# Attention scores of a hybrid decoder's mixer issued in pairs of heads on the two halves of TensorE's rows, with the mixer's order written by hand

## The chip, the core and the metric

The kernel runs on one core of a Trainium2 chip. The metric is the time of one execution on the device in microseconds, lower is better. The core has TensorE (PE) for matmuls, which reads SBUF and writes PSUM, VectorE (DVE), ScalarE (ACT), GpSimd (POOL), and SyncE (SP), which here issues the loads of the weights. Each engine takes its instructions in the order in which the program lists them; between engines, semaphores hold an instruction back until its inputs are there.

## The reference

Two layers, 256 tokens, width 1024, float32. Each layer is a half-step SwiGLU block, a mixer, and a second half-step SwiGLU block; a final RMS norm follows. The change is in the mixer alone:

```python
h = rms_norm(x, norm_mix[l])
qa, ka, va, qb, kb, vb, xc, gc = _split_cols(h @ w_in[l])
# A: 4 query heads, 2 key/value heads of 64, causal window 128, one sink logit per head
out_a = swa_sink_mixer(rope(qa), rope(ka), va, attn_sinks[l])
# B: 6 heads of 64, three dilated windows joined by their softmax denominators
out_b = dilated_mixer(rope(qb), rope(kb), vb)
# C: 384 channels, causal convolution over 4 tokens, gated linear recurrence, times gelu(gc)
out_c = rglru_mixer(xc, gc, conv_w[l], ...)
x = x + concat(out_a, out_b, out_c) @ w_out[l]
```

## The kernel before

Activations stand as columns of tokens in blocks of 128 channels (`xT`), split into a rounded part and a remainder (`hi`, `lo`); a weight piece of up to 128x1024 is loaded by SP into `raw` (`piece`, L123), rounded to `hi` on ScalarE (L130) and its remainder `lo` taken on VectorE (L132). A projection or a feed-forward product is three matmuls for each block of 128 input channels: hi times hi, hi times lo, lo times hi. Five `raw` tiles and fourteen `hi`/`lo` tiles let the weights run ahead of TensorE.

The mixer (L645) is a list of steps, `PLAN` (L20). `xc` and `gc` project C's two branches into channel rows (three PSUM banks each); `qb`, `kb`, `vb` project B's queries, keys and values and `pa` all of A's, with tokens in rows (one bank for each half of the tokens); `cg` and `cs` are C's gates and its recurrence, `co` its last product. `B1s0` is a score step of B for the second half of the tokens (h = 1), `B1p0` the transposes of one tile of probabilities, its copy to SBUF and its products with the values, `B1f` the division by the denominators and the transpose into `PT`; A's steps are named in the same way. `woB` and `woCA` multiply `PT` by `w_out` and add to `xT`. C's `gelu` stands at the end of the step `gc` (L776).

A head has 64 channels, so its scores, `q` times `k`, use 64 of TensorE's 128 rows: even heads of B and A's first key head the lower half, the others the upper half (`g`, L833 to L835). They are plain float32 products and each is recorded as two matmuls (20 head products in a layer, 40 records). A score step takes one PSUM bank (tag `at`) and heads of one half alone; A has two steps for each h, B two for h = 0 and four for h = 1. Then VectorE adds the mask and takes the row maxima (L838), ScalarE takes the exponentials (L847).

The steps are written in the order of `PLAN`, but a scheduler places each engine's instructions: the written order is their priority, and an instruction whose inputs it expects to be late lets later ones pass. `behind(ins)` (L120) pins instructions to come after `ins` on the same engine. PSUM has eight banks: four `mm`, two `at`, two `tp` (transposes). `LO` = 3: the last three input blocks of an output product are taken column block by column block (L941, L942).

Of the kernel before, what the change touches and what calls it, by code (L numbers as in the profile page):

```python
# [11 lines left out]
F32 = mybir.dt.float32  # L12
# [26 lines left out]
def hybrid_trunk(ctx: ExitStack, tc: tile.TileContext, a: dict, out: bass.AP):  # L39
# [397 lines left out]
    def gT(h, g, n, hi, lo):  # L437

        ps = bank("tp", "gT")
        for j in range(n // P):  # L440
            nc.tensor.transpose(ps[:, j * P:(j + 1) * P], g[:, j * P:(j + 1) * P], ident)
        split(hi, lo, ps[:, :n].rearrange("p (k t) -> p k t", t=P))

# [201 lines left out]
    def mixer(l, norm, nxt):  # L645
# [46 lines left out]

        def project(o, n, name):
            bs = None
            for k, w in w_in_pieces(o, n):
                if bs is None:
                    bs = [bank("mm", name)[:, :n] for _ in range(NH)]
                with behind_stats(k):
                    mac([(k, [(norm.parts(h, k), [(bs[h], w)]) for h in range(NH)])], KD)
            return bs  # L700

        def project_T(o, n, name, tags):

            bs = None
            for k, (wh, wl) in w_in_pieces(o, n):
                if bs is None:
                    bs = [bank(t, name)[:, :S] for t in tags]
                xh, xl = (norm.both(k)[:, o:o + S] for o in (0, S))
                with behind_stats(k):
                    for i, b in enumerate(bs):  # L710
                        wi, wj = (p[:, i * P:(i + 1) * P] for p in (wh, wl))
                        nc.tensor.matmul(b, wi, xh, start=(k == 0), stop=False)
                        nc.tensor.matmul(b, wi, xl, start=False, stop=False)
                        nc.tensor.matmul(b, wj, xh, start=False, stop=(k == KD - 1))
# [13 lines left out]
        def c_conv():  # L728
            xc = project_T(oC, CW, "xc", TAG_XC)
# [41 lines left out]
        def c_gelu():  # L771
            gc = project_T(oC + CW, CW, "gc", TAG_GC)
# [3 lines left out]
            A.activation(ge, ge, AF.Gelu_apprx_tanh)  # L776
# [31 lines left out]
        def q_k(ps, h, nh, dst, groups=None):  # L808
            r = rope(ps, h, nh, groups)
            n = nh * HD // P  # L810
            tp = bank("tp", "qkT")
            for c in range(n):
                nc.tensor.transpose(tp[:, c * P:(c + 1) * P], r[:, c * P:(c + 1) * P], ident)
            copy("qk", dst[:, :, h * P:(h + 1) * P], tp[:, :n * P].rearrange("p (c t) -> p c t", c=n))

        class Attend:


            def __init__(self, h, heads, vs, mask, sinks):
                self.h, self.heads, self.vs, self.mask, self.sinks = h, heads, vs, mask, sinks  # L820
                self.nk = (h + 1) * P
                self.nh = sum(len(b) for b in heads)
                st = act.tile([P, 4, 8], F32, tag="st", bufs=4, name="st")
                self.mx, self.nm, self.ls, self.ri = (st[:, i] for i in range(4))
                self.slot = [sum(len(b) for b in heads[:i]) for i in range(len(heads))]
                self.sm = [None] * len(heads)
                self.ob = None

            def scores(self, gi):
                group, j, nk, mx, nm = self.heads[gi], self.slot[gi], self.nk, self.mx, self.nm  # L830
                h, n = self.h, len(group)
# [4 lines left out]
                sm = act.tile([P, 512], F32, tag="sm", bufs=NSM, name="sm")  # L836
                for s in range(n):
                    V.tensor_tensor_reduce(out=sm[:, s * nk:(s + 1) * nk], in0=sb[:, s * nk:(s + 1) * nk],  # L838
                                           in1=self.mask, scale=1.0, scalar=NEG, op0=ALU.add, op1=ALU.max,
                                           accum_out=mx[:, j + s:j + s + 1])  # L840
                if self.sinks is None:
                    V.tensor_scalar(nm[:, j:j + n], mx[:, j:j + n], -SC, None, op0=ALU.mult)
                else:
                    V.scalar_tensor_tensor(nm[:, j:j + n], mx[:, j:j + n], -SC, self.sinks[1][:, j:j + n],
                                           op0=ALU.mult, op1=ALU.min)
                for s in range(n):
                    A.activation(sm[:, s * nk:(s + 1) * nk], sm[:, s * nk:(s + 1) * nk], AF.Exp, scale=SC,  # L847
                                 bias=nm[:, j + s:j + s + 1], accum_out=self.ls[:, j + s:j + s + 1])
                self.sm[gi] = sm

            def pv(self, gi):
                h, sm = self.h, self.sm[gi]
                if self.ob is None:
                    self.ob = bank(TAG_O, "o")
                tp = bank("tp", "pT")
                n = len(self.heads[gi]) * self.nk
                for b in range(n // P):
                    nc.tensor.transpose(tp[:, b * P:(b + 1) * P], sm[:, b * P:(b + 1) * P], ident)
                pT = act.tile([P, 512], F32, tag="pT", bufs=2, name="pT")
                copy("pT", pT[:, :n], tp[:, :n])  # L860
                for s, (i, g, q, k) in enumerate(self.heads[gi]):
                    for kb in range(h + 1):
                        b = s * (h + 1) + kb
                        nc.tensor.matmul(self.ob[:, i * HD:(i + 1) * HD], pT[:, b * P:(b + 1) * P], self.vs[kb][i],
                                         start=(kb == 0), stop=(kb == h))

            def finish(self):
                nh, ls, ri, ob, mx = self.nh, self.ls, self.ri, self.ob, self.mx
                if self.sinks is not None:
                    V.tensor_tensor(mx[:, :nh], self.sinks[0], self.nm[:, :nh], op=ALU.add)  # L870
                    A.activation(mx[:, :nh], mx[:, :nh], AF.Exp)
# [3 lines left out]
                order = [i for group in self.heads for i, *_ in group]  # L875
                if order == list(range(nh)):
                    V.tensor_tensor(o.rearrange("p (n d) -> p n d", d=HD),
                                    ob[:, :nh * HD].rearrange("p (n d) -> p n d", d=HD),
                                    ri[:, :nh, None].to_broadcast([P, nh, HD]), op=ALU.mult)
                else:  # L880

                    v = lambda z: z[:, :nh * HD].rearrange("p (n g d) -> p g n d", g=2, d=HD)
                    V.tensor_tensor(v(o), v(ob), ri[:, :nh].rearrange("p (g n) -> p g n", g=2)[:, :, :, None]
                                    .to_broadcast([P, 2, nh // 2, HD]), op=ALU.mult)
# [8 lines left out]
        def a_in():  # L893
            dst = qkA()
            pa = project(oA, (AQ + 2 * AKV) * HD, "pa")
            for h in range(NH):
# [3 lines left out]
                q_k(pa[h][:, :nq * HD], h, nq, dst, (AKV, AG))  # L900
            C["qkA"] = dst

        def a_attend(h):
# [3 lines left out]
            return Attend(h, heads, va, K["mA"][h], (K["sink"][:, sl], K["nsink"][:, sl]))  # L907

        def b_in(j):
            dst = QB[j][:, :NP * S].rearrange("p (c t) -> p c t", c=NP)  # L910
            pb = project(oB + j * NB, NB, "pb")
# [4 lines left out]
        def b_v():  # L916
            pb = project(oB + 2 * NB, NB, "vb")
# [5 lines left out]
        def b_attend(h, q, k):  # L923
            hd = lambda i: (i, i % 2, q[:, i // 2], k[:, i // 2])
            per = 512 // ((h + 1) * P)
            heads = []
            for g in range(2):
                for i0 in range(0, NP, per):
                    heads.append([hd(2 * i + g) for i in range(i0, min(i0 + per, NP))])
# [101 lines left out]
```

## Time and profile before

| | |
|---|---|
| three runs | 944.31 us median, 944.14 to 946.62 |
| profiled execution | 943.66 us, of which the span of its instructions is 941.9 us |
| PE busy | 933.2 us, 99% of the span, 7572 matmuls |
| DVE busy | 661.7 us, 70% |
| ACT busy | 501.9 us, 53% |
| SP's weight queue (q1) | 168.32 MB, 58.0% of the DMA engines' span |
| PE's granted clock | 0.998 of 2.4 GHz |
| first layer's mixer, first `xc` to last `wout` matmul | 190.15 to 291.08 us |
| second layer's mixer | 651.74 to 752.67 us |

Matmuls are pipelined: the duration of one reaches into the next, so the time that one costs is read from the distance between starts, not from its own duration. In a timeline, a line stands for a run of like instructions (xcount).

### The profile page before, as it was taken

Reading aid. Unit: us, or ns where it says so; the run is one execution under the profiler, and the core shown is the slowest. Engines: PE = TensorE matmul, PEld = TensorE weight load, DVE = VectorE, ACT = ScalarE, POOL = GpSimd, SP = SyncE. Lnnn points to the kernel's source line nnn. Section 1 sums busy time; section 2 is a strip of 40 time slices with the busy share of each in tenths; the row PEclk is TensorE's granted clock in tenths of the full one; section 3 lists DMA queues with packets and bytes.
Section 4 is the critical chain, followed back from the end, with each engine's and each line's share of the span. In section 5 each row is a group of like instructions: output and inputs, shape, how many; then the busy total and the mean of one; then the engine's idle time right before and its main releaser. Section 6 shows DMA issues by size and latency. Waiting matters only on the chain.

```text
span 941.9 us, 18771 instructions
## 1 busy us (share of the span) xinstructions
PE 933.2 (99%) x7572; PEld 908.8 (96%) x7572; DVE 661.7 (70%) x1155; ACT 501.9 (53%) x769; POOL 60.2 (6%) x107
## 2 busy tenths in 40 slices
PE   9999999999999999999999999999999999999997
PEld 8999999999899999999999999999988999999886
DVE  6787766999678767766477767565995975656544
ACT  7545554555577545554455545444475675555530
POOL 4000001011102000001000000011100100000000
PEclk9999999999999999999999999999999999999999
DMA  8886674665246665565756666654741755665631
GB/s 287 235 250 193 180 220 148 187 188 154 79 146 202 196 205 183 180 222 167 215 159 202 201 206 195 203 178 121 224 137 46 234 180 180 197 207 201 202 112 45
DMA packets 134406, 171.13 MB, mean 182 GB/s; under 512 B 5820, under 2 KB 106256, under 8 KB 134320
## 3 DMA queue, kind: packets, MB, share of 16 engines
q1 hardware_dynamic: 133184, 168.32, 58.0%
q0 software_dynamic: 528, 0.57, 0.5%
q8 instruction: 59, 0.97, 0.4%
q10 hardware_dynamic: 608, 1.06, 0.3%
q14 instruction: 27, 0.22, 0.1%
HBM read 168.88 MB, written 1.05 MB: 180 GB/s over the span
## 4 chain that ended last, share of the span: by engine, by line
PE 98%; issue 1%; DMA 1%; SPq 0%; DVE 0%; POOLq 0%; POOL 0%
PE gate L467 9%; PE gate L468 8%; PE gate L469 8%; PE up L467 8%; PE up L469 8%; PE up L468 8%; PE down L468 6%; PE down L467 6%; PE down L469 6%; PE down L616 2%; PE down L615 2%; PE down L617 2%; PE scores L834 2%; PE wout L946 2%; PE wout L947 2%; PE wout L948 2%
## 5 line engine op out<-in xcount | busy, mean ns | idle before, releaser
L132 DVE TENSOR_TENSOR lo<-raw,hi 128x1024 fp32r<-128x1024 f32 (+2 forms) x334 | 388.6, 1173 | 113.5 <-ACT hi L130 113.2
L130 ACT ACTIVATE hi<-raw 128x1024 fp32r<-128x1024 f32 (+2 forms) x334 | 335.6, 1018 | 167.0 <-PE down L468 60.9
L467 PE MATMUL gate<-x,hi 128*128 128x256 f32 x704 | 194.7, 277 | 0.1
L468 PE MATMUL gate<-x,hi 128*128 128x256 f32 x704 | 193.9, 276 | 0.0
L467 PE MATMUL up<-x,hi 128*128 128x256 f32 x704 | 193.6, 275 | 0.0
L468 PE MATMUL up<-x,hi 128*128 128x256 f32 x704 | 193.5, 275 | 0.0
L469 PE MATMUL gate<-x,lo 128*128 128x256 f32 x704 | 193.3, 275 | 0.0
L469 PE MATMUL up<-x,lo 128*128 128x256 f32 x704 | 193.3, 275 | 0.0
L467 PE MATMUL down<-g,hi 128*128 128x256 f32 x528 | 145.3, 275 | 0.0
L468 PE MATMUL down<-g,hi 128*128 128x256 f32 x528 | 145.2, 275 | 0.0
L469 PE MATMUL down<-g,lo 128*128 128x256 f32 x528 | 145.1, 275 | 0.0
L467 PEld LDWEIGHTS gate<-x,hi 128*128 128x128 f32 x704 | 132.3, 188 | 0.4 <-ACT x L376 0.4
L468 PEld LDWEIGHTS gate<-x,hi 128*128 128x128 f32 x704 | 132.2, 188 | 0.0
L468 PEld LDWEIGHTS up<-x,hi 128*128 128x128 f32 x704 | 132.1, 188 | 0.0
L469 PEld LDWEIGHTS up<-x,lo 128*128 128x128 f32 x704 | 132.1, 188 | 0.0
L467 PEld LDWEIGHTS up<-x,hi 128*128 128x128 f32 x704 | 132.0, 188 | 0.0
L469 PEld LDWEIGHTS gate<-x,lo 128*128 128x128 f32 x704 | 131.9, 188 | 0.0
L136 ACT ACTIVATE g<-gu 128x256 fp32r<-128x256 f32 x88 | 36.6, 418 | 148.3 <-DVE gu L481 124.5
L467 PEld LDWEIGHTS down<-g,hi 128*128 128x128 f32 x528 | 99.1, 188 | 0.1
L468 PEld LDWEIGHTS down<-g,hi 128*128 128x128 f32 x528 | 99.1, 188 | 0.0
L469 PEld LDWEIGHTS down<-g,lo 128*128 128x128 f32 x528 | 99.0, 188 | 0.0
L480 DVE TENSOR_TENSOR gu<-up,half 128x256 f32<-128x256 f32 x66 | 27.7, 420 | 46.1 <-PE up L469 46.0
(228 smaller groups left out, 1323.8 us busy)
## 6 DMA issues: line engine op xcount, KB each, us to landing
raw<-ffn_down SPq DMA_DIRECT2D x88, 512.0 KB, 4.6
raw<-ffn_gate SPq DMA_DIRECT2D x87, 512.0 KB, 4.8
raw<-ffn_up SPq DMA_DIRECT2D x87, 512.0 KB, 5.0
raw<-w_in SPq DMA_DIRECT2D x40, 384.0 KB, 3.8
raw<-w_out SPq DMA_DIRECT2D x12, 512.0 KB, 3.7
raw<-w_in SPq DMA_DIRECT2D x8, 512.0 KB, 4.8
raw<-w_out SPq DMA_DIRECT2D x8, 256.0 KB, 2.8
xr<-x SPq DMA_DIRECT2D x4, 256.0 KB, 4.2
```

Of the source, the lines that this page charges most:

```text
L130: nc.scalar.activation(hi[:, :m], raw[:, :m], AF.Copy)
L132: nc.vector.tensor_tensor(lo[:, :m], raw[:, :m], hi[:, :m].bitcast(F32), op=ALU.subtract)
L136: nc.scalar.activation(hi, v, AF.Copy)
L467: nc.tensor.matmul(b, wh, both[:, :S], start=first, stop=False)
L468: nc.tensor.matmul(b, wh, both[:, S:], start=False, stop=False)
L469: return nc.tensor.matmul(b, wl, both[:, :S], start=False, stop=last)
L480: V.tensor_tensor(u, bs[1], half, op=ALU.mult)
L615: nc.tensor.matmul(b, gh, wh, start=first, stop=False)
L616: nc.tensor.matmul(b, gh, wl, start=False, stop=False)
L617: return nc.tensor.matmul(b, gl, wh, start=False, stop=last)
L834: nc.tensor.matmul(sb[:, s * nk:(s + 1) * nk], q[g * HD:(g + 1) * HD, h * P:(h + 1) * P], k[g * HD:(g + 1) * HD, :nk], start=True, stop=True)
L946: nc.tensor.matmul(bs[j], wi, PT[:, k, 0], start=(i == 0), stop=False)
```

## The change

Scores: a step takes two `at` banks, one for each half of the rows, and goes through its heads by turns, lower half, upper half (`banks`, a list of two lists of heads). A has one such step for each h, B one for h = 0 (three pairs) and two for h = 1 (two pairs, then one): five steps in a layer instead of ten. The tiles of probabilities are filled by head number, so B has two and three of them, A one and two. The sink's exponential is taken at the end of A's score step instead of in `finish`.

Order: the step `p` is taken apart into `p` (transposes and copy) and `o` (products with the values). Projections, and `out_stage`, are generators that stop after two input blocks, or between their parts; each naming in `PLAN` runs one part. `C["pe"]` holds the last matmul so far of the projections and output products (or of a `gT`), and scores, transposes and value products are pinned behind it. A's query and key transposes (`aT0`, `aT1`) leave `a_in`, which now comes ahead of `vb`. The gelu is a step of its own (`gl`), pinned on ScalarE behind the last exponential of A. `o` tiles move from `at` to `mm`; an output product has two banks of each.

The core of the diff (left out: `whole`, which runs a generator to its end; `to_channels`, split from `q_k`; the same `yield` and `C["pe"]` in `project_T`; the regrouping of heads in `a_attend` and `b_attend`; `go_on`, which runs a step's next part):

```diff
-PLAN = ("xc qb kb cg B1s0 vb B0s0 B0s1 B0p0 B0p1 pa B1s2 B1s1 cs A0s0 B1s3 B1p0 B0f A0s1 B1p2 B1p1 A1s0 B1p3 "
-        "A1s1 A0p1 A0p0 gc A1p0 B1f woB A1p1 A0f A1f co woCA").split()
-TAG_GATE, TAG_SCORES, TAG_O, TAG_WO = 'at', 'at', 'at', 'mm'
-TAG_XC, TAG_GC = ('mm', 'at', 'mm'), ('at', 'mm', 'mm')
+PLAN = ("xc qb kb cg pa pa pa B0s0 pa B1s0 vb B0p0 B0p1 B1s1 cs vb aT0 vb aT1 A0s0 vb gc B0o0 B0o1 B1p0 B1p1 "
+        "gc B1o0 B1o1 B1p2 B0f gc B1o2 A0p0 gc B1f A0o0 A1s0 gl woB A1p0 A1p1 A0f woB A1o0 A1o1 co "
+        "woCA A1f woCA woCA woCA").split()
+TAG_GATE, TAG_SCORES, TAG_O, TAG_WO = 'at', 'at', 'mm', ('mm', 'mm', 'at', 'at')
+TAG_XC, TAG_GC = ('mm', 'at', 'mm'), ('mm', 'mm', 'mm')
...
         def project(o, n, name):
...
             for k, w in w_in_pieces(o, n):
+                if k and k % 2 == 0:
+                    yield
...
-                    mac([(k, [(norm.parts(h, k), [(bs[h], w)]) for h in range(NH)])], KD)
+                    C["pe"] = mac([(k, [(norm.parts(h, k), [(bs[h], w)]) for h in range(NH)])], KD)
...
         def c_gelu():
-            gc = project_T(oC + CW, CW, "gc", TAG_GC)
+            gc = yield from project_T(oC + CW, CW, "gc", TAG_GC)
...
-            A.activation(ge, ge, AF.Gelu_apprx_tanh)
...
             def scores(self, gi):
-                sb = bank(TAG_SCORES, "scores")
-                for s, (i, g, q, k) in enumerate(group):
-                    nc.tensor.matmul(sb[:, s * nk:(s + 1) * nk], q[g * HD:(g + 1) * HD, h * P:(h + 1) * P],
-                                     k[g * HD:(g + 1) * HD, :nk], start=True, stop=True)
+                sb = [bank(TAG_SCORES, "scores") for _ in banks]
+                for s in range(max(len(b) for b in banks)):
+                    for t, group in zip(sb, banks):
+                        if s < len(group):
+                            i, g, q, k = group[s]
+                            at[i] = t[:, s * nk:(s + 1) * nk]
+                            with behind(C["pe"]):
+                                nc.tensor.matmul(at[i], q[g * HD:(g + 1) * HD, h * P:(h + 1) * P],
+                                                 k[g * HD:(g + 1) * HD, :nk], start=True, stop=True)
...
+                if self.sinks is not None:
+                    V.tensor_tensor(mx[:, sl], self.sinks[0][:, sl], nm[:, sl], op=ALU.add)
+                    C["exp"] = A.activation(mx[:, sl], mx[:, sl], AF.Exp)
+
+            def pT(self, gi):
+                sm, heads = self.sm[gi]
+                tp = bank("tp", "pT")
+                n = len(heads) * self.nk
+                for b in range(n // P):
+                    with behind(C["pe"]):
+                        nc.tensor.transpose(tp[:, b * P:(b + 1) * P], sm[:, b * P:(b + 1) * P], ident)
...
         def out_stage(ks, last):
             for c in range(HC):
+                if c:
+                    yield
...
-                for i, j in order:
+                for ij, (i, j) in enumerate(order):
+                    if ij and ij == (n - LO) * KC:
+                        yield
...
+            elif nm == "gl":
+                with behind(C["exp"]):
+                    A.activation(C["ge"], C["ge"], AF.Gelu_apprx_tanh)
+            elif nm == "aT":
+                h = int(arg)
+                to_channels(C["rA"][h], h, nq, C["qkA"], C["pe"])
```

## Rows read from the trace of the kernel before

**Rows 1.** Waits of PE over the whole span: total us, times, longest.

```profile
PE warm L115 <- POOL ident masks.py:199: 1.4, 1, 1.4
PE xT L371 <- DMA xr<-x: 0.6, 1, 0.6
```

**Rows 2.** The page's part 4, the chain that ended last, by engine.

```profile
PE 98%; issue 1%; DMA 1%; SPq 0%; DVE 0%; POOLq 0%; POOL 0%
```

**Rows 3.** Groups by form, the score matmuls: xcount | busy us, mean ns.

```profile
L834 PE MATMUL scores<-mixed 64*128 64x256 f32 x40 | 11.8, 407 | 0.0
...
L834 PE MATMUL scores<-mixed 64*128 64x128 f32 x40 | 6.4, 287 | 0.0
```

**Rows 4.** PE's timeline at B0s1: start us, us, instruction.

```profile
238.51 0.40 PE L431 MATMUL pa<-hi,x 128*128 128x512 f32 x1
238.84 0.93 PE L834 MATMUL scores<-mixed 64*128 64x128 f32 x6
239.70 0.50 PE L432 MATMUL pa<-lo,x 128*128 128x512 f32 x1
240.04 0.40 PE L434 MATMUL pa<-hi,x 128*128 128x512 f32 x1
240.27 0.39 PE L431 MATMUL pa<-hi,x 128*128 128x512 f32 x1
```

**Rows 5.** PE's timeline at B1s2 and at B1s1.

```profile
247.59 1.13 PE L834 MATMUL scores<-mixed 64*128 64x256 f32 x4
248.65 0.88 PE L864 MATMUL o<-vb,pT 128*128 128x64 f32 x6
...
252.01 0.70 PE L834 MATMUL scores<-mixed 64*128 64x256 f32 x2
252.64 0.38 PE L712 MATMUL gc<-x,hi 128*128 128x256 f32 x1
```

**Rows 6.** PE's timeline: a run of output matmuls, and A's last scores.

```profile
255.80 1.61 PE L864 MATMUL o<-vb,pT 128*128 128x64 f32 x13
257.25 0.39 PE L858 MATMUL pT<-ident,sm 128*128 128x128 f32 x2
...
261.06 1.13 PE L834 MATMUL scores<-mixed 64*128 64x256 f32 x4
```

**Rows 7.** Busy us of each engine, by stretch, then PEclk, DMA share, GB/s.

```profile
190.15:291.08 100.93, 100.93 (x705) 94.20 (x704) 84.32 (x187) 61.63 (x120) 13.84 (x13) 1.00 0.50 152
...
215.00:225.00 10.00, 10.00 (x58) 9.57 (x58) 9.99 (x17) 6.88 (x11) 2.02 (x2) 1.00 0.47 134
225.00:235.00 10.00, 10.00 (x51) 8.54 (x50) 9.80 (x22) 4.92 (x6) 0.00 (x0) 1.00 0.47 149
...
265.00:275.00 10.00, 10.00 (x90) 10.00 (x89) 8.33 (x14) 9.01 (x15) 0.00 (x0) 1.00 0.49 138
```

**Rows 8.** ScalarE's timeline from A's last exponentials to the split of C.

```profile
264.20 0.50 ACT L847 ACTIVATE sm<-sm,st 128x256 f32<-128x256 f32 x1
...
264.69 0.50 ACT L847 ACTIVATE sm<-sm,st 128x256 f32<-128x256 f32 x1
...
265.76 1.58 ACT L130 ACTIVATE hi<-raw 128x512 fp32r<-128x512 f32 x2
267.35 1.28 ACT L776 ACT_TABLE_LOAD   x1
268.65 0.85 ACT L776 ACTIVATE ge<-ge 128x768 f32<-128x768 f32 x1
...
270.87 0.83 ACT L136 ACTIVATE parts<-ge 128x768 fp32r<-128x768 f32 x1
```

**Rows 9.** VectorE's timeline of the same chain.

```profile
262.23 0.42 DVE L838 CUSTOM_DVE_ANT_0 sm<-scores,mA 128x256 f32<-128x256 f32 x1 [0.61 <-PE scores L834]
...
262.57 0.42 DVE L838 CUSTOM_DVE_ANT_0 sm<-scores,mA 128x256 f32<-128x256 f32 x1
...
272.81 0.95 DVE L137 TENSOR_TENSOR parts<-ge,parts 128x768 fp32r<-128x768 f32 x1
```

More of the change, by code (lines that the diff above doesn't have):

```diff
@@ L435, in mac, with gT @@
         return last
-    def gT(h, g, n, hi, lo):
+    def gT(h, g, n, hi, lo, after=None):
         ps = bank("tp", "gT")
         for j in range(n // P):
-            nc.tensor.transpose(ps[:, j * P:(j + 1) * P], g[:, j * P:(j + 1) * P], ident)
+            with behind(after):
+                last = nc.tensor.transpose(ps[:, j * P:(j + 1) * P], g[:, j * P:(j + 1) * P], ident)
         split(hi, lo, ps[:, :n].rearrange("p (k t) -> p k t", t=P))
+        return last
     OFF, NTAIL = 4, 40
@@ L691, in behind_stats, with whole @@
             return behind(C.get("stats"))
+        def whole(g):
+            while True:
+                try:
+                    next(g)
+                except StopIteration as e:
+                    return e.value
         def project(o, n, name):
@@ L821, in __init__ @@
                 self.nk = (h + 1) * P
-                self.nh = sum(len(b) for b in heads)
+                self.nh = sum(len(b) for banks, _ in steps for b in banks)
                 st = act.tile([P, 4, 8], F32, tag="st", bufs=4, name="st")
                 self.mx, self.nm, self.ls, self.ri = (st[:, i] for i in range(4))
-                self.slot = [sum(len(b) for b in heads[:i]) for i in range(len(heads))]
-                self.sm = [None] * len(heads)
+                self.sm, self.p = [], {}
@@ L836, in scores @@
[L836 to L840, printed above, removed]
+                (banks, tiles), nk, mx, nm, h = self.steps[gi], self.nk, self.mx, self.nm, self.h
@@ new lines, in scores @@
+                p = {}
+                for tile_heads in tiles:
+                    sm = act.tile([P, 512], F32, tag="sm", bufs=NSM, name="sm")
+                    p.update((i, sm[:, s * nk:(s + 1) * nk]) for s, i in enumerate(tile_heads))
+                    self.sm.append((sm, tile_heads))
+                order = [i for t in tiles for i in t]
+                for i in order:
+                    V.tensor_tensor_reduce(out=p[i], in0=at[i], in1=self.mask, scale=1.0, scalar=NEG, op0=ALU.add,
+                                           op1=ALU.max, accum_out=mx[:, i:i + 1])
@@ L853, in pv @@
                 if self.ob is None:
                     self.ob = bank(TAG_O, "o")
[L855 to L861, printed above, removed]
+                for s, i in enumerate(heads):
@@ L874, in finish @@
                 o = scratch(nh * HD, "o")
[L875 to L884, printed above, removed]
+                V.tensor_tensor(o.rearrange("p (n d) -> p n d", d=HD),
+                                ob[:, :nh * HD].rearrange("p (n d) -> p n d", d=HD),
+                                ri[:, :nh, None].to_broadcast([P, nh, HD]), op=ALU.mult)
                 return o
@@ L958, in out, with go_on @@
         def out(stage):
-            out_stage([R[m] for m in stage], stage == PLAN[-1][2:])
+            return out_stage([R[m] for m in stage], stage == PLAN[-1][2:])
+        running = {}
+        def go_on(step, start):
+            if step not in running:
+                running[step] = start()
+            next(running[step], None)
         for step in PLAN:
```

84 lines of the change are left out of this document (47 added, 37 removed).

## The prediction

> **What bounds the kernel now.** I read the waits of PE first. In the whole span it waits twice, 1.4 and 0.6 us, both at the start [rows 1]; the chain of waits says the same, 98% of it is PE [rows 2]. In a stretch of the mixer PE is busy for all of its 10 us, at the full granted clock, while VectorE is at 8 to 10 us and ScalarE at 5 to 9 [rows 7]. So the time is the sum of the distances between the starts of PE's instructions, and a change gains what it takes out of that sum, less any wait that it opens. A first mixer lasts 100.93 us [rows 7], and the second one repeats it; I work out one layer and double.
>
> **What the scores cost now.** There are 40 records of 256 columns and 40 of 128 in the kernel [rows 3], so 20 and 20 in a layer. Their durations overlap, so I take starts. A run of four wide ones takes 248.65 - 247.59 = 1.06 us to the start of the next work, a run of two 252.64 - 252.01 = 0.63 [rows 5]: one costs (1.06 - 0.63)/2 = 0.215, and 0.20 is left over once in each run. Six narrow ones take 239.70 - 238.84 = 0.86 [rows 4]; less 0.20 that is 0.11 each. The neighbours pay too: the projection's matmuls stand 240.27 - 240.04 = 0.23 apart, but the step into the run is 238.84 - 238.51 = 0.33, and the first step behind it 240.04 - 239.70 = 0.34. A run of scores thus costs 0.10 + 0.20 + 0.11 = 0.41 beside its matmuls, half of it at each edge: PE passes between 64 and 128 rows. PE's timeline has nine such runs in a layer (B1s0 and B0s0 stand in one). One layer: 20 x 0.215 + 20 x 0.11 + 9 x 0.41 = 6.5 + 3.7 = 10.2 us.
>
> The Trainium skill, "TensorEngine Tiling (Array Packing)", Key Properties, says that changing the tiling mode drains TensorE and that changing only the tile does not. The trace agrees on the first, with 0.41 for in and out; no run here shows the second, and the last rival below hangs on it.
>
> **Part 1, fewer runs.** Ten steps become five, and with transposes and outputs pinned around them I count five runs. Four runs less are 4 x 0.41 = 1.64 us a layer, 3.3 in all. All of it lies on PE's path.
>
> **Part 2, pairs on two halves.** The trace of before has no upper-half score directly behind a lower-half one in PE's order, so the overlap is not shown and is bounded. Each head is two matmuls, and they keep their order: lower, lower, upper, upper. At best the second of a head runs beside the first of the next: a pair takes two times instead of four, and the first time of a run stays uncovered. With T = 0.11 or 0.215 that is 7T for B0 (three pairs), 5T for A0, 5T for B1s0 and for A1s0, 3T for B1s1: 0.77 + 0.55 + 1.08 + 1.08 + 0.65 = 4.1 instead of 6.5, 2.4 less. At worst short of a loss the pairs stand one behind another, 0 less. Between them stands the weight load. Thirteen value products, which stream only 64 columns, take 257.25 - 255.80 = 1.45 us, 0.11 each [rows 6], as much as a score with twice the columns: a load sets their pace, one for each 0.11. If the two halves share that, a pair needs at least 4 x 0.11 = 0.44 us. That is the 0.44 that a narrow pair costs now, but half of the 0.86 of a wide one. I take this value, since its row is of this kernel and nearest: narrow 2.2, wide 1.08 + 1.08 + 0.65 = 2.8, together 5.0, so 1.5 us less a layer and 3.0 in all. For the range I keep 0 and 4.7 (twice 6.5 - 4.13), and 1.0 more if the 0.10 of the second matmul in each of ten runs is hidden by the other half.
>
> **Part 3, the tail.** What does PE do while C's branch ends? In the order written out, `woCA` starts with C's rows of `PT`, and these come from A's exponentials by a chain with nothing beside it: the gelu is pinned behind them on ScalarE, and `co` and the split are queued behind the gelu on VectorE and ScalarE. Before, the chain from A's last scores at 261.06 [rows 6] to the end of C's remainder at 272.81 + 0.95 = 273.76 [rows 9] lasted 12.7 us: reduces 0.34 apart [rows 9], exponentials 0.49 apart, table load 1.28, gelu 0.85, split 0.83 [rows 8]. In the new step four heads go through instead of two: 2 x 0.34 + 2 x 0.49 = 1.7 more, 14.4. The two roundings of `w_out` ahead of the table load, 1.58 us [rows 8], now come behind `gl` in the written order: 12.8. The cover on PE, from the start of A1s0: its own 5 x 0.215 + 0.3 = 1.4; 72 matmuls of `woB` at 10/90 = 0.11 [rows 7], 8.0; eight transposes and the two of A0f, 1.1; sixteen value products, 1.8. Sum 12.3. PE is short of 0.5 us a layer, 1.0 in all. Ends: 0, if VectorE and ScalarE serve the chain at once, and 14.4 - 12.3 = 2.1 a layer, if roundings stand in it as before.
>
> **Edits costed at nothing.** VectorE loses some small reductions of maxima and ScalarE two probability copies a layer; neither is late [rows 1]. `pa` comes ahead of `vb`, with its loads: SP's order is changed with PE's, the bytes stay, and DMA engines are at half share in the mixer [rows 7]. A's rotary work and transposes fall into the stretch in which VectorE has 19.8 of 20 us (215 to 235) [rows 7] but PE has up to seven pieces of weights in hand; what hides it is that C's recurrence may slip, needed only at `co`. If that cover is gone, one late remainder costs about 0.95 (a row of 768 columns [rows 9]), two a layer 3.8 in all. The third bank of `gc` waits for the copy of `vb`, since two banks of `vb` and three of `gc` exceed four; matmuls to the first two banks stand ahead of it. A score step waits for both `at` banks, hence for four reduces, 4 x 0.34; a part of a projection lies between two B steps.
>
> **The sum.** -3.3 - 3.0 + 1.0 = -5.3 against the profiled execution's 943.66: 938.4. The median of the runs, 944.31, lies 0.65 above that one: **939.0 us**.
>
> **Rivals.**
> Both halves load and multiply at the same time: 4.7 instead of 3.0 from part 2, 943.66 - 3.3 - 4.7 + 1.0 + 0.65 = 937.3. For it: the operands of two halves share no rows. Against it: the pace of loads in [rows 6]. The same page of the Trainium skill, Key Properties, says that different tiles execute loads and matmuls in parallel; by that rule this rival would hold, and no run here shows it. Chance 0.25.
> Loads go strictly in order, each behind the start of the matmul ahead of it: then each change of half leaves a load of 0.11 bare, a wide pair costs 2 x 0.215 + 0.22 = 0.65 instead of 0.86, a narrow one gains nothing. A wide run of two pairs is 1.40 instead of 1.72, one of one pair 0.75 instead of 0.86: 0.75 a layer, 1.5 in all: 940.5. Chance 0.15.
> The change doesn't do what it says, pairs run one after another and only part 1 is left: 943.66 - 3.3 + 1.0 + 0.65 = 942.0. Chance 0.10.
> The tail is the bound: 2.1 a layer of waiting for the gelu chain, 943.66 - 6.3 + 4.2 + 0.65 = 942.2. For it: ScalarE has 9.0 of 10 us in 265 to 275 [rows 7]. Against it: `gl` stands ahead of the roundings. Chance 0.07.
> Slower: TensorE drains at each change of half as it does at a run's edge, 0.41/2 = 0.20. A layer has 5 + 3 + 3 + 1 + 3 = 15 such changes, 3.1 us against 1.64 saved; it decides from 1.64/15 = 0.11 a change. Both layers lose 2.9, with the tail's 1.0: 943.66 + 3.9 + 0.65 = 948.2. For it: the only changes of rows in the trace cost that much. Against it: those change the number of rows, these do not. Chance 0.08.
>
> **Chances and range.** The forecast holds 0.35, the five rivals 0.65 as given. A measurement here can tell about 0.3%, 2.8 us, from no change. Faster by more (under 941.5): the forecast, both halves at once and loads in order, 0.75, less 0.05 for a tail near its upper end, 0.70. Slower by more (over 947.1): the drain, and 0.02 for no overlap with late remainders, 0.10. The rest, 0.20, within. The range goes from both halves at once without a wait and with the hidden 0.10s, 944.31 - 9.0 = 935.3, to loads in order with the whole tail, 944.31 - 4.8 + 4.2 = 943.7.
>
> **What would show it.** Starts of scores: upper and lower beside each other (two starts within some 10 ns, a pair of 256 columns in about 0.43 us), narrow pairs at 0.44 if loads are shared, 0.22 if not, 0.65 for a wide pair if loads go in order, and 0.2 at each change if it drains. Five runs a layer with 0.41 each. PE's waits: none in the mixer but up to 0.5 us each before the first `woCA` matmul, released by C's remainder (`parts`). The mixer should last 100.93 - 2.6 = 98.3 us. The prediction is wrong if PE waits elsewhere, for `vb`'s copy or a late remainder, or if runs of scores are cut into more than five.

## The result, and the profile after

| | before | changed |
|---|---|---|
| median | 944.24 us (944.14 to 946.62, 4 runs) | 937.21 us (936.94 to 938.74, 4 runs) |
| ratio | | 0.9923, interval 0.9904 to 0.9942 |
| profiled execution, span | 943.66, 941.9 | 936.94, 935.2 |
| first `xc` to last `wout` matmul, layer 1 | 100.93 | 98.08 |
| first `xc` to the first `down` of the next block, layer 1 | 221.49 | 218.01 |

The change makes the kernel faster by 7.0 us, 0.8%. 939.0 had been forecast. All through this part the time of a stretch is a distance between starts, and since the changed mixer has eight matmuls of the next block's gate and up projections before its last `wout` matmul, the longer stretch of the last line is the fair one: 3.48 us less a layer, 7.0 in both. Executions of most of these kernels fall on two levels some 1.7 us apart, which by the kept traces differ at the program's start (first `xc` at 190 to 191 us, or at 192 to 193) and not in the mixers; so medians closer than that are read together with this stretch.

PE's waits in the changed kernel (total us, times, longest), which answer to [rows 1]: all three are at the start, none is listed in a mixer.

```profile
PE warm L116 <- POOL ident masks.py:199: 1.4, 1, 1.4
PE gate L470 <- ACT x L377: 0.9, 1, 0.9
PE xT L372 <- DMA xr<-x: 0.7, 1, 0.7
```

The mixer of the changed kernel (stretch, us; then the busy us of PE, PEld, DVE, ACT, POOL with their instructions; then PEclk, DMA share, GB/s), as in [rows 7]. PE is still without a gap and at its full clock.

```profile
190.34:288.42 98.08, 98.08 (x714) 92.31 (x713) 83.03 (x181) 60.95 (x118) 15.83 (x13) 1.00 0.50 153
```

Groups by form of the changed kernel (xcount | busy us, mean ns), as in [rows 3]. The records are as many as before and nearly as long each, yet their busy time together fell from 18.2 to 10.6 us: they now lie over one another.

```profile
L858 PE MATMUL scores<-mixed 64*128 64x256 f32 x40 | 7.3, 407 | 0.0
L858 PE MATMUL scores<-mixed 64*128 64x128 f32 x40 | 3.3, 292 | 0.0
```

PE's timeline of the changed kernel (start us, us, instruction) at the score runs of layer 1, which answers to [rows 4, 5].

```profile
227.97 0.40 PE L435 MATMUL pa<-hi,x 128*128 128x512 f32 x1
228.30 0.94 PE L858 MATMUL scores<-mixed 64*128 64x128 f32 x12
229.17 0.50 PE L432 MATMUL pa<-hi,x 128*128 128x512 f32 x1
...
234.94 1.14 PE L858 MATMUL scores<-mixed 64*128 64x256 f32 x8
236.01 0.44 PE L433 MATMUL vb<-lo,x 128*128 128x384 f32 x1
...
242.19 0.70 PE L858 MATMUL scores<-mixed 64*128 64x256 f32 x2
242.81 0.44 PE L433 MATMUL vb<-lo,x 128*128 128x384 f32 x1
...
244.03 0.70 PE L858 MATMUL scores<-mixed 64*128 64x256 f32 x2
244.65 0.55 PE L832 MATMUL qkT<-ident,r 128*128 128x128 f32 x3
```

Three things are to be seen. Twelve narrow matmuls take 229.17 - 228.30 = 0.87 us, where six took 0.86 [rows 4]. Eight wide ones take 236.01 - 234.94 = 1.07, where four took 1.06 [rows 5]. And B's last pair, written as one step, stands as two runs of two (242.19 and 244.03): six runs a layer, not five. The two other runs are eight narrow matmuls for A and the first half of the tokens (0.65 us) and the eight wide ones for A and the second half (1.07, below).

The starts within a run are plainer still. These are those of the twelve narrow matmuls from 228.30 on, in us after 228, with the next projection matmul last:

```
.298 .304  .511 .518  .623 .629  .734 .741  .846 .853  .958 .964  1.166
```

Six pairs, the two of a pair 6 or 7 ns apart, the pairs 0.11 apart: the pace that single ones had. The first 0.21 of a run holds the 0.10 left over at its start, and its matmul is paired like the rest.

### The profile page after: what moved, and what is told of

Read it like the earlier page. It is cut to its first block, busy times and chain, and to the rows that moved or that the text cites. A ratio compares the mean times of both kernels' runs of the same rounds, so it can differ in the third digit from the quotient of the medians.

```text
span 935.2 us, 18754 instructions
## 1 busy us (share of the span) xinstructions
PE 925.4 (99%) x7572; PEld 902.4 (96%) x7572; DVE 661.1 (71%) x1145; ACT 499.5 (53%) x765; POOL 65.1 (7%) x107
## 3 DMA queue, kind: packets, MB, share of 16 engines
q10 hardware_dynamic: 608, 1.06, 0.4%
## 4 chain that ended last, share of the span: by engine, by line
PE 95%; issue 2%; POOL 1%; DVE 1%; DMA 1%; ACT 0%; SPq 0%; POOLq 0%; ACTq 0%; DVEq 0%
PE up L472 8%; PE up L470 8%; PE up L471 8%; PE gate L470 8%; PE gate L472 8%; PE gate L471 8%; PE down L470 6%; PE down L472 6%; PE down L471 6%; PE down L620 2%; PE down L619 2%; PE down L618 2%; PE wout L981 1%; PE wout L982 1%; PE o L899 1%
```

## The experiments

### Both heads of a pair on the same half

Is it the two halves, or only the smaller number of runs and the new order?

```diff
                             i, g, q, k = group[s]
+                            g = 0
```

> The changed kernel, but every head's scores read the lower 64 rows (the upper heads' scores are thus those of their lower neighbours); order, banks, pins and counts stay. Theory A (the gain is the two halves working at the same time): a layer's scores take 20 x 0.215 + 20 x 0.11 = 6.5 us of starts instead of the 3.7 seen, 2.8 more, 5.6 in all: 937.2 + 5.6 = 942.8. Rival B (the gain is the smaller number of runs and the order by hand, the overlap counts for little): within 1 us of 937.2.

Measured: 942.53 us (941.67 to 944.58, 10 runs), ratio to before 0.9981 (0.9972 to 0.9990). PE's timeline of this kernel at the first two score runs:

```profile
228.96 1.60 PE L859 MATMUL scores<-mixed 64*128 64x128 f32 x12
230.49 0.50 PE L432 MATMUL pa<-hi,x 128*128 128x512 f32 x1
...
236.27 1.99 PE L859 MATMUL scores<-mixed 64*128 64x256 f32 x8
238.19 0.44 PE L433 MATMUL vb<-lo,x 128*128 128x384 f32 x1
```

Twelve narrow matmuls now take 1.53 us (0.87 in the changed kernel), eight wide ones 1.92 (1.07). Summed from start to start, a layer's scores take 7.71 us here and 4.90 in the changed kernel, the 2.8 that theory A gave; `wout` takes 0.21 less here, so the stretch to the next `down` is 2.5 us longer in each layer. The halves alone are worth 942.53 - 937.21 = 5.3 us by the medians, 5.0 by the stretches. What stays without them, fewer runs and the new order less what these cost, is 944.23 - 942.53 = 1.7 us.

### All heads of one half, then all of the other

How far ahead of its place in the written order may the other half start?

```diff
-                for s in range(max(len(b) for b in banks)):
-                    for t, group in zip(sb, banks):
+                first = C["pe"]
+                for t, group in reversed(list(zip(sb, banks))):
+                    for s in range(max(len(b) for b in banks)):
...
-                            with behind(C["pe"]):
-                                nc.tensor.matmul(at[i], ...
+                            with behind(first):
+                                first = nc.tensor.matmul(at[i], ...
```

> The changed kernel, but a score step writes all its upper heads and then all its lower ones, in one piece. If each half of the rows takes its matmuls from a queue of its own, whatever the written order (theory A), nothing is lost by this, and B1s1's pair, now in one run, gains 0.43 + 0.41 a layer: 937.2 - 1.7 = 935.5. If a matmul can't start before the one written ahead of it (rival C), a run of n heads in each half overlaps by one matmul time alone: 5T lost in B0, 3T in A0, B1s0 and A1s0, 5 x 0.11 + 3 x 0.11 + 6 x 0.215 = 2.2 us a layer, 4.3 in all, less the 1.7: 939.8.

Measured: 938.38 us (936.33 to 938.59, 4 runs), ratio 0.9931 (0.9917 to 0.9944); the stretches to the next `down` are 217.61 and 219.58 us, 0.4 and 0.3 shorter than in the changed kernel, since B's last pair is one run again (0.63 us at 246.14). Neither theory's time came.

Two heads behind two others (B's step at 238.01) overlap in full, 1.07 us as in the changed kernel. Three behind three (230.69) take 1.19 instead of 0.87. Their starts, in us after 230, with the next projection matmul last:

```
.688  .902  1.013 1.019  1.125  1.233 1.237  1.344 1.348  1.456  1.568  1.679  1.881
```

On one half (the run above) no two matmuls start closer than 0.1 us, so of two that start 4 to 6 ns apart one is the other half's: its first one, seventh in the written order, begins beside the third start, and needs some 0.21 to its second as the first of a run does. If each half keeps its own order, one half starts at .688, .902, 1.013, 1.125, 1.233 and 1.344, the other at 1.019, 1.237, 1.348, 1.456, 1.568 and 1.679; which start is whose the trace does not say. So the halves need not alternate to overlap, but with six matmuls ahead of it the other half began two of them, 0.33 us, late, and with four ahead not at all.

### The upper head first in each pair

The changed kernel lets the scheduler place the heads of a step. This one chains them, the upper head of a pair first.

```diff
+                first = C["pe"]
                 for s in range(max(len(b) for b in banks)):
-                    for t, group in zip(sb, banks):
+                    for t, group in reversed(list(zip(sb, banks))):
...
-                            with behind(C["pe"]):
-                                nc.tensor.matmul(at[i], ...
+                            with behind(first):
+                                first = nc.tensor.matmul(at[i], ...
```

> The changed kernel, but in each score step the head of the upper half is written first and the next ones are pinned behind it, so that the pair of B1s1 stands in one run: five runs a layer instead of six, and that pair overlaps. Theory A: 0.43 + 0.41 a layer less, 1.7 in all: 935.5. If the split of that pair costs nothing (rival B): 937.2.

Measured: 936.04 us (935.84 to 937.51, 5 runs), ratio 0.9915 (0.9901 to 0.9928), the lowest median of all. PE's timeline of this kernel at B's last pair:

```profile
243.57 0.70 PE L859 MATMUL scores<-mixed 64*128 64x256 f32 x4
244.20 0.66 PE L832 MATMUL qkT<-ident,r 128*128 128x128 f32 x4
```

The pair is one run of 0.63 us again, in place of two of 0.62, and the layer has five runs. Joining them saves 0.41 for the run and 0.43 of overlap, 0.84; the stretch to the next `down` fell by 0.70, from 218.01 to 217.31. In the second layer it fell by 0.36 only. Beside the changed kernel the gain is 1.2 us of medians, and the intervals of the two ratios overlap; that it is faster rests on the stretches of its one trace.

### Pairs in the old order, without pins

Is the order written by hand needed at all?

```diff
-PLAN = ("xc qb kb cg pa pa pa B0s0 pa B1s0 vb B0p0 B0p1 B1s1 cs vb aT0 vb aT1 A0s0 vb gc B0o0 B0o1 B1p0 B1p1 "
...
+PLAN = ("xc qb kb cg B1s0 vb vb vb vb B0s0 B0p0 B0o0 B0p1 B0o1 pa pa pa pa aT0 aT1 B1s1 cs A0s0 B1p0 B1o0 B0f "
+        "B1p2 B1o2 B1p1 B1o1 A1s0 A0p0 A0o0 gc gc gc gc gl A1p0 A1o0 B1f woB woB A1p1 A1o1 A0f A1f co "
+        "woCA woCA woCA woCA").split()
...
-                            with behind(C["pe"]):
+                            with behind(None):
```

(and the same for transposes, value products, `gl` and `aT`.)

> Pairs alone: the step list follows the order of the kernel before, projections whole, no step pinned behind another, gelu without its pin; scores in pairs on two halves as in the change. Theory A: the scores keep the gain (10.2 us a layer before, 3.3 to 3.7 of matmuls and 0.41 for each of three to six runs now, so 4.5 to 6.2), 944.2 - 2 x 4.0 to 944.2 - 2 x 5.7 = 936.2 to 932.8, less whatever waits the order brings. Rival B: without the order by hand there is little left, 942 or more.

Measured: 996.8 us (991.42 to 999.03, 4 runs), ratio 1.0546 (1.0516 to 1.0576). The largest of PE's waits in this kernel, its timeline behind `vb`, and a stretch:

```profile
PE scores L858 <- DVE st L867: 11.4, 4, 5.3
```

```profile
230.06 1.13 PE L858 MATMUL scores<-mixed 64*128 64x256 f32 x8
235.05 2.34 PE L858 MATMUL scores<-mixed 64*128 64x128 f32 x12 [3.85 <-DVE st L867]
238.53 2.43 PE L858 MATMUL scores<-mixed 64*128 64x256 f32 x4 [1.14 <-DVE st L867]
```

```profile
234.00:246.00 12.00, 9.81 (x33) 6.93 (x34) 7.03 (x34) 8.50 (x28) 0.00 (x0) 0.50 0.07 22
```

A step of pairs holds both `at` banks until VectorE has reduced them. Here three steps come one behind another in PE's order, with no projection between, and the second and the third wait for the reduces (`st`, L867) of the one before. The clock makes it worse: it fell during the wait of 3.85 us and stood at 0.50 of the full one, 1.2 GHz, from 234 to 246. A run of twelve narrow matmuls lasted 2.34 us instead of 0.94; its halves did not start in pairs either (first starts 235.05, 235.42, 235.63), so the clock is not all of it. In this order the pairs lacked work of another kind between them. This kernel changes the order and the pins together, so what each costs it does not tell.

### The new order without the pins

```diff
-                            with behind(C["pe"]):
+                            with behind(None):
```

(scores, transposes, value products, `aT` and `gT`; the gelu's pin stays.)

> The changed kernel without the pins on TensorE (scores, transposes, value products and gT are not held behind the last projection matmul or gT); the gelu keeps its pin. By the instruction lists TensorE's order changes at one place of each layer: A's second scores pass ahead of B's last transposes (gT). Theory A (the pins only confirm what the scheduler does): 937.2, within 0.6. Rival D (holding A's second scores behind B's transposes is worth something, since woB waits for the latter): the gT and its split come 0.86 + 0.41 = 1.3 us later and the first woB matmul waits for it; A0's eight value products, 0.9 us, hide part: 0.4 to 1.3 a layer, 938.0 to 939.8.

Measured: 940.03 us (939.18 to 941.29, 4 runs), ratio 0.9946 (0.9930 to 0.9963); the stretch to the next `down` is 219.12 and 220.99 us in the two layers, 1.1 longer than in the changed kernel in each. PE's timeline of this kernel:

```profile
262.03 1.13 PE L858 MATMUL scores<-mixed 64*128 64x256 f32 x8
263.09 0.55 PE L443 MATMUL gT<-ident,o 128*128 128x128 f32 x3
...
265.08 0.38 PE L981 MATMUL wout<-parts,hi 128*128 128x256 f32 x1 [0.19 <-DVE st L867]
265.76 0.38 PE L981 MATMUL wout<-parts,hi 128*128 128x256 f32 x1 [0.30 <-DVE st L867]
266.23 0.39 PE L982 MATMUL wout<-parts,hi 128*128 128x256 f32 x1
```

and VectorE's:

```profile
265.63 0.55 DVE L138 TENSOR_TENSOR parts<-gT,parts 128x384 fp32r<-128x384 f32 x1
```

In the changed kernel the three transposes of B (`gT`) stand ahead of A's second scores (259.78 and 260.19, below). Without the pins the scores pass them, B's remainder comes to stand behind the scores' reduces on VectorE (265.63), and the first matmuls of `woB` wait. Two of these waits end with the reduces themselves: L981 reads the rounded part alone, but the third and fourth output bank of `woB` are the `at` banks that A's scores hold until they are reduced. L982, which reads the remainder, follows as soon as that is done. PE's order differs elsewhere too, in where A's transposes stand among the `wout` matmuls, but `wout` has 1.0 of the 1.1 us (23.93 instead of 22.93 from start to start). So holding A's second scores behind B's transposes is worth about 1 us a layer. It is the pin that does it: the written order is the same in both kernels.

### The gelu in its old place

```diff
-        "gc B1o0 B1o1 B1p2 B0f gc B1o2 A0p0 gc B1f A0o0 A1s0 gl woB A1p0 A1p1 A0f woB A1o0 A1o1 co "
+        "gc B1o0 B1o1 B1p2 B0f gc B1o2 A0p0 gc B1f A0o0 A1s0 woB A1p0 A1p1 A0f woB A1o0 A1o1 co "
...
+            A.activation(ge, ge, AF.Gelu_apprx_tanh)
```

(at the end of the step `gc`, without a pin.)

> The changed kernel with the gelu back at the end of the step that projects gc, ahead of A's last exponentials, without a pin. ScalarE then loads the gelu's table, and the exponentials' one again: 1.28 us more in each layer, and A's last exponentials come 2 x 1.28 + 0.85 = 3.4 us later. Theory A (the tail has its slack on the side of C, 0.3 us at most, and more on the side of A's outputs): A's value products come later, and PE fills with woB, 937.2 within 0.6. Rival E (A's chain is as tight as C's): up to 3 us a layer of waits, 943.

Measured: 936.89 us (936.79 to 938.55, 4 runs), ratio 0.9920 (0.9905 to 0.9935); stretches 217.94 and 219.83, beside 218.01 and 219.88. Holding the gelu behind A's exponentials, which is a part of the change, is worth nothing that can be measured.

### A longer chain behind A's exponentials

How much slack has the tail? Three copies of `ge` onto itself are added behind the gelu on ScalarE.

```diff
                     A.activation(C["ge"], C["ge"], AF.Gelu_apprx_tanh)
+                    for _ in range(3):
+                        A.activation(C["ge"], C["ge"], AF.Copy)
```

> The changed kernel with three more passes of ScalarE over the gelu's result (a copy onto itself, about 0.76 us each from start to start), so C's chain is 2.3 us longer. In the changed kernel's trace C's remainder is done 0.3 us ahead of the first woCA matmul. If that is all the slack: 2.0 us a layer of waiting, 4.0 in all, 941.2. If A's value products and transposes can fill it, less: 937.2 to 939.

Measured: 950.52 us (948.37 to 951.19, 4 runs), ratio 1.0056 (1.0040 to 1.0073), far over the 941.2 that was expected if the slack was 0.3; stretches 5.2 and 5.6 us longer than in the changed kernel, in an execution (948.37) that was the shortest of the four. ScalarE's timeline of this kernel from the gelu on, then PE's, then a stretch:

```profile
268.67 0.85 ACT L1025 ACTIVATE ge<-ge 128x768 f32<-128x768 f32 x1
...
270.37 0.83 ACT L1027 ACTIVATE ge<-ge 128x768 f32<-128x768 f32 x1
...
275.25 1.06 ACT L131 ACTIVATE hi<-raw 128x1024 fp32r<-128x1024 f32 x1
276.52 0.84 ACT L137 ACTIVATE parts<-ge 128x768 fp32r<-128x768 f32 x1 [0.21 <-DVE ge L796]
```

```profile
277.42 1.32 PE L981 MATMUL wout<-parts,hi 128*128 128x256 f32 x6 [2.94 <-ACT parts L137]
279.21 0.58 PE L982 MATMUL wout<-parts,hi 128*128 128x256 f32 x1 [0.47 <-DVE parts L138]
...
280.23 0.41 PE L982 MATMUL wout<-parts,hi 128*128 128x256 f32 x1
280.44 0.41 PE L983 MATMUL wout<-parts,lo 128*128 128x256 f32 x1
```

```profile
278.00:281.00 3.00, 2.53 (x12) 2.23 (x12) 1.16 (x2) 0.00 (x0) 0.00 (x0) 0.50 0.70 213
```

The three copies, the first at 270.37, are 2.3 us of work, yet from the gelu to the split it is 7.85 us (268.67 to 276.52), and 2.70 in the changed kernel (267.94 to 270.64), 5.2 less: between the copies stand more roundings of weights (such as 275.25) and a copy of A's transposes, which in the changed kernel come behind the split. PE then waited 2.94 and 0.47 us, 3.4 of the 5.2. Most of the rest is clock, some 1.4 us (`wout` took 1.87 more from start to start, of which 0.47 was the wait): it stood at 0.50 of full speed, 1.2 GHz, from 278 to 281, and matmuls of `wout` came 0.21 apart (280.23, 280.44) instead of 0.11. The tail's slack is small, and a wait there costs more than its length.

### Two steps in one run

Built on the kernel with the upper head first: B's last pair is written into the free 256 columns of the two banks of A's first step, as one run.

```diff
-PLAN = ("xc qb kb cg pa pa pa B0s0 pa B1s0 vb B0p0 B0p1 B1s1 cs vb aT0 vb aT1 A0s0 vb gc B0o0 B0o1 B1p0 B1p1 "
+PLAN = ("xc qb kb cg pa pa pa B0s0 pa B1s0 vb B0p0 B0p1 cs vb aT0 vb A0s0 aT1 vb gc B0o0 B0o1 B1p0 B1p1 "
...
-                sb = [bank(TAG_SCORES, "scores") for _ in banks]
+                sb, c0 = share or ([bank(TAG_SCORES, "scores") for _ in banks], 0)
+                C["sb"] = sb, c0 + 256
```

> As upper_first, and B1s1's two heads are written into the free 256 columns of the two banks of A0s0, directly behind A's four heads, so that a layer has four runs of scores instead of five: 0.41 a layer less than upper_first, 0.8 in all: 936.0 - 0.8 = 935.2. If a run's edges cost nothing beside their neighbours (rival B): 936.0.

Measured: 937.36 us (935.65 to 937.39, 4 runs), ratio 0.9917 (0.9902 to 0.9931); stretches 217.05 and 219.43, against 217.31 and 219.53 with the upper head first. Four runs instead of five should give 0.41 a layer; 0.26 and 0.10 came. PE waits for B's values ahead of their transposes:

```profile
PE gT L443 <- DVE o L915: 0.4, 2, 0.2
```

Part of the gain went into that wait, 0.2 a layer; in the second layer two steps between matmuls of `gc` also take 0.65 us together (704.53 to 705.18) instead of 0.23, for a reason that isn't shown. The medians don't tell the two kernels apart.

### B's transposes earlier

Also built on the kernel with the upper head first, in which one step between two `woB` matmuls still takes 0.38 us instead of 0.11.

```diff
-        "gc B1o0 B1o1 B1p2 B0f gc B1o2 A0p0 gc B1f A0o0 A1s0 gl woB A1p0 A1p1 A0f woB A1o0 A1o1 co "
+        "gc B1o0 B1o1 B1p2 B0f gc B1o2 B1f A0p0 gc A0o0 A1s0 gl woB A1p0 A1p1 A0f woB A1o0 A1o1 co "
```

> The upper head of each pair goes first, as in the run upper_first (936.0), and B's transposes of the last two heads (B1f) are written ahead of the last piece of the gates (gc). Theory A: in upper_first the first matmul of B's output projection waited some 0.3 us a layer, because B's remainder on VectorE came behind a rounding remainder of the gate. With the transposes earlier the remainder is issued earlier, that wait goes, and the time is 936.04 - 2*0.27 = 935.5. Theory B: the wait moves to the transposes themselves, which now wait for B's values to be normalised, and the time stays at 936.0 or rises to 936.5.

Measured: 938.03 us (937.79 to 939.45, 5 runs), ratio 0.9930 (0.9916 to 0.9944); both theories missed. PE's and VectorE's timelines of this kernel:

```profile
259.29 1.14 PE L859 MATMUL scores<-mixed 64*128 64x256 f32 x8
260.35 0.55 PE L443 MATMUL gT<-ident,o 128*128 128x128 f32 x3
...
262.43 0.35 PE L982 MATMUL wout<-parts,hi 128*128 128x256 f32 x1 [1.09 <-DVE st L868]
```

```profile
262.89 0.55 DVE L138 TENSOR_TENSOR parts<-gT,parts 128x384 fp32r<-128x384 f32 x1
```

The transposes were written earlier and came later. With another piece of `gc` written behind them, A's scores are pinned behind that piece and no longer behind the transposes, and pass them. B's remainder then stands behind A's four reduces (262.89), and the first `woB` matmul is one for an `at` bank, which A's scores hold until they are reduced; it reads the rounded part alone (L982 here), and its wait of 1.09 us ends with the reduces, ahead of the remainder. It is the same fault as without pins, made by a step moved, and its price is the same: stretches 218.19 and 220.38, 0.9 us longer than with the upper head first.

## Why the prediction was right, and where its steps were off

The sign and the range held: 937.2 lies between 935.3 and 943.7. The forecast itself, 939.0, was 1.8 too high, and the first rival, both halves at once, describes what happened. That its 937.3 lies so close is luck: it had 4.7 for the pairs and 3.3 for the runs, where 5.6 and 2.5 came. Step by step, in us over both layers:

| step | forecast | in the trace |
|---|---|---|
| part 1, fewer runs | -3.3 (nine to five a layer) | -2.5 (nine to six) |
| part 2, pairs on two halves | -3.0 | -5.6 |
| part 3, the tail | +1.0 | none before `woCA`; +1.1 about `wout` |
| sum | -5.3 | -7.0 |

The last column is counted from single runs and steps. Summed from start to start, a layer's stretch to the next `down` has 8.29 us of scores before and 4.90 now, 22.29 and 22.93 of `wout`, and 0.73 less of all the rest, where three runs' edges outside the scores would be 0.63: together the 3.48.

**What the scores cost now** held. The runs of the changed kernel's first layer, in PE's order, take 0.87 + 1.07 + 0.62 + 0.62 + 0.65 + 1.07 = 4.90 us together, of which 6 x 0.20 belongs to the runs and 3.70 to matmuls; with single times of 0.11 and 0.215, twenty narrow ones in ten times and twenty wide ones in twelve (of which the cut pair takes four) give 1.1 + 2.6 = 3.7. The edges held too: the step into a run is 0.33 (227.97 to 228.30), 0.10 more than the projection's 0.23 [rows 4]. The prediction put the whole edge on the passage between 64 and 128 rows, and for the step behind a run that isn't shown: behind value products and transposes, which use all 128 rows, the first `wout` matmul takes 0.09 longer too (part 3), nearly the 0.11 behind a run of scores. Both are plain float32 work ahead of rounded products; no run separates the two causes.

**Part 2** is the step that failed, and it failed by its size. Two assumptions in it did not hold. That a load's pace of 0.11 is shared by the halves: it isn't, narrow pairs stand 0.11 apart, two loads in 0.11. That the two matmuls of a head keep their order, so that the other half begins beside the second one: it begins beside the first, and no first time stays uncovered. Hence not even the 5.0 us that a layer's matmuls were given, but 3.70, below the best case of 4.13. The run on one half put a price on all of it that owes nothing to this sum: 5.3 us. The value products of [rows 6], from which the load's pace was taken, use all 128 rows, so they never showed what two halves can do; they were the nearest rows, and the nearest rows answered another question. The Trainium skill, "TensorEngine Tiling (Array Packing)", Key Properties, says that different tiles load and multiply in parallel, and here the trace agrees in full: eight matmuls in 1.07 us where four took 1.06. The rival that rested on it had 0.25.

**The rival of a drain at each change of half** fell with it: fifteen changes a layer would have cost 3.1 us, and the pairs show none. Loads in order (0.65 for a wide pair) and pairs one after another fell as well; the latter is what the run on one half does by force, and its 942.5 stands beside the 942.0 given for it.

**Part 1** was off by one run, and the prediction had named that (more than five runs) as a sign of being wrong. B's last pair was cut, 0.43 of overlap lost and 0.41 for the run. VectorE's timeline of the changed kernel shows what both its banks had to wait for:

```profile
239.25 0.42 DVE L867 CUSTOM_DVE_ANT_0 sm<-scores,mB 128x256 f32<-128x256 f32 x1
...
239.60 1.54 DVE L784 TENSOR_TENSOR_SCAN mixed<-mixed 128x256 f32<-128x256 f32 x2
...
241.39 0.41 DVE L867 CUSTOM_DVE_ANT_0 sm<-scores,mB 128x256 f32<-128x256 f32 x1
```

The step before freed one bank at 239.7 and, with two scans of C's recurrence between, the other at 241.8. The scheduler placed the head of the first bank at 242.19 and let others pass before that of the second. In the trace both were free by 242.19, so PE was held by the order that the scheduler had set, not by a bank. That the late bank is the reason is argued from these rows; that a chain of the heads mends it is shown by the run with the upper head first, where PE's waits still name none in a mixer. The prediction had named both banks and the full VectorE, under the edits costed at nothing, and looked for a wait. The price came as a run cut in two, with no idle time at all, which the waits cannot show.

**Part 3.** No wait opened before `woCA`, and that +1.1 came where +1.0 had been forecast is chance: it is another cost. PE's, ScalarE's and VectorE's timelines of the changed kernel, as in [rows 6, 8, 9]:

```profile
259.78 0.49 PE L443 MATMUL gT<-ident,o 128*128 128x128 f32 x3
260.19 1.13 PE L858 MATMUL scores<-mixed 64*128 64x256 f32 x8
261.26 1.10 PE L899 MATMUL o<-va,pT 128*128 128x64 f32 x8
262.17 0.60 PE L981 MATMUL wout<-parts,hi 128*128 128x256 f32 x3
262.69 0.39 PE L982 MATMUL wout<-parts,hi 128*128 128x256 f32 x1
...
273.71 0.48 PE L981 MATMUL wout<-parts,hi 128*128 128x256 f32 x2
274.03 0.28 PE L982 MATMUL wout<-parts,hi 128*128 128x256 f32 x1
```

```profile
267.94 0.85 ACT L1025 ACTIVATE ge<-ge 128x768 f32<-128x768 f32 x1
...
270.64 0.84 ACT L137 ACTIVATE parts<-ge 128x768 fp32r<-128x768 f32 x1
```

```profile
262.09 0.55 DVE L138 TENSOR_TENSOR parts<-gT,parts 128x384 fp32r<-128x384 f32 x1
...
272.43 0.95 DVE L138 TENSOR_TENSOR parts<-ge,parts 128x768 fp32r<-128x768 f32 x1
```

The chain from A's scores to the end of C's remainder lasted 272.43 + 0.95 - 260.19 = 13.2 us, between the 12.8 and 14.4 forecast. The cover was 273.71 - 260.19 = 13.5, not 12.3: the sum had left out A's eight value products of the first half (261.26, 0.9 us), which PE's order has behind these scores. So 0.3 us remain to the `woCA` matmul at 273.71 and 0.65 to the first one that reads the remainder, L982 at 274.03; the longer chain shows how little that is. What the step did not have is a cost about `wout` itself. B's remainder, at 262.09, came as the first `woB` matmuls ran, and from the third of them (262.50) over 262.69 to the one behind it (262.91) two steps take 0.41 instead of 0.23: 0.18. And `woB` is now broken up by more transposes and value products: the first `wout` matmul behind such work takes 0.20 to the next start instead of 0.11, eight times a layer where it was four: 4 x 0.09 = 0.36. Together 0.54 a layer, the 1.1 of the table.

**The edits costed at nothing** opened no wait that the profile lists: the order of the loads, the copy of `vb` and C's recurrence made nobody late, although VectorE was busy for the whole of 225 to 245. **What would show it** named 98.3 us for the mixer (98.08, with some 0.9 of the next block in it) and 0.44 or 0.22 for a narrow pair (0.22).

What stays open: the second layer gained only half as much as the first from the upper head first, 0.36 us instead of 0.70. Of the 0.34 between them 0.12 lies in the pair itself: its run takes 0.75 us (from 700.98), and its second half starts 0.12 behind the first, at 701.11, just after the last reduce of the step before (to 701.05). Another 0.19 lies in the matmuls of `gc`; why is not shown, nor what held `gc` in the shared run.

## What to carry to other kernels

Float32 products with 64 rows to contract that come one behind another on one half leave the other half idle: give each half a PSUM bank and put heads of both into one run, and the second half's matmuls cost nothing. Such a step holds twice the banks: three of them with nothing between waited 11.4 us in two layers for VectorE, so place other work of PE between two. Where a scheduler orders the engine, chain what must stay together: read the run lengths in the timeline beside the waits, since a run cut in two shows no idle time. Before moving a step, look at which instruction its neighbours were pinned behind: a later piece of work can take over the pin and let through what it was to hold back.

## What the runs showed of the hardware

Where nothing holds one of them back, matmuls of the two halves start 4 to 14 ns apart and share nothing that these runs can see: neither the time of the columns (eight wide in 1.07 us) nor the pace of the loads (twelve narrow in 0.87).

The two halves don't follow one common order of starts. In A's first step of the changed kernel the heads stand in the program as lower, lower, upper, upper, two matmuls each, and these start as `.733 .746  .946 .959  1.058 1.071  1.169 1.183` (us after 247), in pairs from the first; with six matmuls of one half ahead, the other half's first one began beside the third start and not behind the sixth. The Trainium skill, "TensorE: Matmul & The Clock Gate", Part 3, What overlaps and what doesn't, says that matmuls start and end strictly in program order; for matmuls on different halves the starts here speak against it.

A wait cost more than its length. After 2.94 us of waiting the granted clock was 0.50 for 3 us and matmuls of 256 columns stood 0.21 apart instead of 0.11; in the kernel with pairs in the old order it fell to 0.50 during a wait of 3.85 us and stayed there until 246, though PE had no gap from 240 on.
